# A hybrid attention and retention block on one Trainium2 core: small transposes and products of ones replaced by DMA, first MLP blocks reordered

## The chip, the cores and the metric

The kernel runs on one core of one Trainium2 chip. The metric is the device time of one execution in microseconds (us). TensorE (PE) multiplies, VectorE (DVE) and ScalarE (ACT) work on rows, GpSimd (POOL) and SyncE (SP) here only issue DMAs.

## The reference, cut to what matters

One layer, 256 tokens, model width 2048, float32. An indexer with 16 heads of 64 picks 64 keys for every query of an attention with 16 heads; beside it runs a retention with 8 heads; both are gated, merged, projected, and an MLP of width 8192 follows.

```python
h = rms_norm(x, ln1_g[l])
proj = h @ w_in[l]                       # queries, keys, values, indexer, retention, gates ga, gb
...
logits = jnp.einsum('bqhd,bsd->bqhs', iqb, ik)                     # indexer
score = jnp.einsum('bqh,bqhs->bqs', iwb, jax.nn.relu(logits))
_, idx = lax.top_k(score, topk)
...
merged = jax.nn.sigmoid(ga) * (o_attn @ w_up_attn[l]) + jax.nn.sigmoid(gb) * (o_ret @ w_up_ret[l])
x = x + merged @ w_out[l]
h2 = rms_norm(x, ln2_g[l])
x = x + jnp.square(jax.nn.relu(h2 @ w_ff1[l])) @ w_ff2[l]
```

## The kernel before, in words

All weights stream through once, in a fixed order (`stream`, `use`). A weight item is a tile of 2 x 128 rows and 512 columns. ScalarE rounds it to a shorter float format (`whi`, L363) and VectorE subtracts to get the rest (`wlo`, L364). Each float32 product is three TensorE products (L409 to L411): high by high, high by low, low by high. `ahead` issues loads on SP's queue eight items before their use and splits two or three items before; `lows` lists the subtractions made so far, `late["split"]` the newest rounding.

Tokens lie in two tiles (t = 0, 1) of 128. `run_block` goes through the 16 steps (k) of a block of 512 columns; at each step `step()` lets all small pieces of work in the list `work` advance by one `yield`. So the number of yields in a generator sets how many steps lie between its parts. The scheduler of the language then places instructions on each engine in its own order; `tc.issue_after(i)` keeps an instruction behind i on its engine.

The blocks in order: keys of the attention together with the indexer's first block, the indexer's other two (`I`), values (`AV`), queries (`AQ`), retention queries and keys (`RQ`, `RK`), the gates `GA` and `GB` (in seven products of quarter blocks instead of eight, `PRODUCTS`, with `SUMS` of weight tiles made on VectorE and `TIED` naming those that are kept behind a subtraction; between them stand items of other blocks), `RG`, `RV`, `UR`, the output projection `O`, then the MLP: `F1` for the first group of 1024 hidden columns as two plain blocks (1, then 0), and for seven more groups as seven products each, between items of `F2`.

A tile is turned (transposed) in two ways. On TensorE by a product with the identity, as in `indexer` (L579, L584) and `last_rows` (L1139), with an eviction from PSUM. Or by DMA (`turned`): ScalarE splits float32 into two planes of 16 bits (L451), SP issues a transposing DMA (L453), and ScalarE joins the planes some steps later (L457).

Three places spread one number per token over all partitions or columns. `forms_h` builds sums of the two token tiles for the gates; it needs the ratio of the tiles' norm factors, `rho`, as a row on every partition: a diagonal matrix times ones (L764). `spread_rs` does the same for the factors of the second norm (L1181), used by `scaled_rows`, which scales the transposed rows of blocks 0 to 2 of `O`. The last block's rows go through `last_rows`, which scales them on ScalarE before the transposes. `next_norm` then splits them into `xf`, which the `F1` blocks read, and `forms` builds four more combinations and holds the tile `rawc` for it, into which `F2` weights are loaded afterwards.

The attention's `attend_tile` waits for `keys`, made at the end of `indexer`. The gates' values are made by sigmoids on ScalarE (L500); `gated` (L904) multiplies them with the attention's projection. A sigmoid of a dummy tile (L835) stands after the second `RQ` block.

Of the kernel before, what the change touches and what calls it, by code (L numbers as in the profile page):

```python
# [10 lines left out]
F32 = mybir.dt.float32  # L11
# [66 lines left out]
def stream():  # L78
# [25 lines left out]
    for g in range(NG):  # L104
# [15 lines left out]
        15: ("C", "A", 0), 18: ("C", "A", 1), 22: ("D", "C", 0), 25: ("D", "C", 1)}  # L120
TIED = {(("GA", 0), ("A", "B", 1)): 4, (("GA", 0), ("B", "C", 0)): 8, (("GA", 1), ("B", "C", 0)): 2, (("GA", 1), ("B", "C", 1)): 4, (1, ("B", "C", 0)): 4, (1, ("C", "A", 0)): 4}
F2_HALVES = (1, 0)
# [17 lines left out]
PAIR = (("UR", 0), ("UR", 1))  # L140
PARTS = ((0, 1), (2,), (3,))

BESIDE = {"GA": "UA", "GB": "RG"}
# [18 lines left out]
def block_kernel(ctx, tc, cst, rot, xt, gains, w, x, ret_gn_g, ret_gn_b, out):  # L162
# [29 lines left out]

    W_NORM, W_SOFT, W_GN, W_CROSS, W_ROWS, W_LAST, W_QUERY, W_PROBS = 3, 5, 7, 8, 7, 6, 5, 5
    n_stg, n_mid, n_sm = 8, {"ep": 12, "e4": 20}, 24
# [64 lines left out]
    for key, name, _, nk, _, n in stream():  # L259
        B[key] = (nk, n)  # L260
        for h in range(nk // KC):
            at[key, h] = (w[off:off + KC * P * n].rearrange("(p c n) -> p c n", p=P, c=KC), n)
            if name != "w_ff2" and key[0] not in QUARTERS and key[0] not in BESIDE.values() and key not in PAIR:
# [183 lines left out]
    def turned(src, halves, wait, tied=False, dst=None, mirror=None):  # L447

        mirror = src if mirror is None else mirror
        with tc.issue_after(late["split"]) if tied else nullcontext():  # L450
            nc.scalar.activation(planes(halves), interleaved(src), AF.Copy)  # L451
        yield
        nc.sync.dma_start_transpose(mirror.bitcast(U16).rearrange("p (c r) -> p c r", r=P), halves.bitcast(U16))  # L453
        for _ in range(wait):
            yield
        with tc.issue_after(late["split"]):
            nc.scalar.activation(interleaved(halves if dst is None else dst), planes(mirror), AF.Copy)  # L457

# [100 lines left out]

    iqs = ep.tile([P, T, IW], F32, tag="big", name="iqs")  # L560
    for i in range(3):
        ps = run_block(("I", i), of(hT)) if i else psI
        for t in range(T):
            evict(iqs[:, t, i * IN:(i + 1) * IN], ps[t], t)
    mb = []

    def indexer():
        ik2 = mid([P, T, 2, ID])
# [3 lines left out]
        iqT = ep.tile([P, IH // 2, S], F32, tag="a1", name="iqT")  # L572
        ikT = mid([P, S])
        yield
        for c in range(0, IH // 2, 2):
            ps = psum_t()
            for a in range(2):
                for t in range(T):
                    nc.tensor.transpose(ps[:, (2 * a + t) * P:(2 * a + t + 1) * P], iqs[:, t, (c + a) * P:(c + a + 1) * P], ident)  # L579
            nc.scalar.activation(iqT[:, c:c + 2, :], ps.rearrange("p (a s) -> p a s", a=2), AF.Copy)  # L580
            yield
# [3 lines left out]
        nc.vector.tensor_copy(ikT, ps[:, :S])  # L585
        yield
        yield
# [16 lines left out]
        sc = [mid([P, (t + 1) * P]) for t in range(T)]  # L604
        for t, h0 in ((0, 0), (1, 0), (1, IH // 2)):
            heads = logits(t, h0)
            yield
            for h, src in enumerate(heads, h0):
                if h == 0:
                    nc.vector.tensor_scalar(sc[t], src, iw[:, t, h:h + 1], None, op0=ALU.mult)  # L610
                else:
                    nc.vector.scalar_tensor_tensor(sc[t], src, iw[:, t, h:h + 1], sc[t], op0=ALU.mult, op1=ALU.add)
                if h % 4 == 3:
                    yield
# [3 lines left out]
        for i in range(TOPK // 8):  # L618
            m8 = [small(8) for _ in range(T)]
            for t in range(T):  # L620
                nc.vector.max(m8[t], sc[t])
            for t in range(T):
                nc.vector.match_replace(sc[t], m8[t], sc[t], GONE)
            yield
            if i % 2:
                yield
        for t in range(T):
# [132 lines left out]
    def forms_h():  # L760

        diag, ps = stage((P, P)), psum_t()
        nc.vector.tensor_scalar(diag, ident, rho, None, op0=ALU.mult)
        nc.tensor.matmul(ps[:, :P], warm, diag, start=True, stop=True)  # L764
        nc.scalar.activation(ratio, ps[:, :P], AF.Copy)
        yield
# [13 lines left out]
        for half in range(2):  # L780
            whole(X2[:, half], 1, half)
            yield
            for q in range(0, HK, 4):
# [28 lines left out]
    for which, key in ((0, "RQ"), (1, "RK")):  # L812
        for i in range(2):
            last = (which, i) == (1, 0)
            ps = run_block((key, i), of(hT), before=(lambda k: scaled(k // 4 - 1) if k in (4, 8, 12) else None) if last else None)
            if which == i == 0:
# [9 lines left out]
                late["rtab"] = e2.tile([P, 2, T, 2, RD], F32, name="rtab")  # L826
                late["rawc"] = px.tile([P, 2, KC, BN], F32, tag="big2", name="rawc")
                nc.gpsimd.dma_start(late["rtab"].rearrange("p a b c d -> p (a b c d)"), rot)
            for t in range(T):
                work.append(rotated(evicted(ps[t], t), t, which, i))  # L830
            if which == i == 0:
                work.append(forms_h())
            if (which, i) == (0, 1):
                with tc.issue_after(late["split"]):
                    nc.scalar.activation(small(8), warm[:, :8], AF.Sigmoid)  # L835
            if last:
# [62 lines left out]
    def gated(u, done, ready):  # L899

        for t, i in list(ready):
            if done[i] == DK // HC:
                z = ready.pop((t, i))
                nc.vector.tensor_tensor(z, acc[2 * u + i][t], z, op=ALU.mult)  # L904
                nc.gpsimd.dma_start(mgd[:, t, (2 * u + i) * BN:(2 * u + i + 1) * BN], z)
# [200 lines left out]

    crossed = [0] * 3

    def cross(i, t):

        for _ in range(2 + t):
            yield
# [12 lines left out]

    def last_rows(i):

        xs = []
        for t in range(T):
            a = stage()  # L1130
            nc.scalar.activation(a, x2[:, t, i * BN:(i + 1) * BN], AF.Copy, scale=rs[:, t:t + 1])
            xs.append(a)
        yield
        half, c0 = divmod(4 * i, HK)
        for k in range(0, 4, 2):
            ps = psum_t()
            for c in range(2):
                for t in range(T):
                    nc.tensor.transpose(ps[:, (2 * c + t) * P:(2 * c + t + 1) * P], xs[t][:, (k + c) * P:(k + c + 1) * P], ident)  # L1139
            for c in range(2):  # L1140
                nc.scalar.activation(xr[half][:, :, c0 + k + c, :], ps[:, c * S:(c + 1) * S].rearrange("p (t s) -> p t s", t=T),
                                     AF.Copy, scale=g2[:, 4 * i + k + c:4 * i + k + c + 1])
            yield

    def next_norm(i):

        yield from scaled_rows(i) if i < 3 else last_rows(i)
        yield
# [24 lines left out]
    def spread_rs():  # L1173

        diag = stage((P, S))
        for t in range(T):
# [4 lines left out]
        nc.tensor.matmul(ps[:, :S], warm, diag, start=True, stop=True)  # L1181
        nc.scalar.activation(across, ps[:, :S], AF.Copy)
        late["across"] = across.rearrange("p (t s) -> p t s", t=T)
# [24 lines left out]
    def norm_end():  # L1208
# [7 lines left out]
        nc.vector.tensor_tensor(q2, rec, rec, op=ALU.mult)  # L1216

    work.append(norm_end())

# [26 lines left out]
    ys = {}  # L1246
    for i in (1, 0):
        ps = run_block(("F1", i), lambda k, t: form(blocks[k // HK][t], k % HK))
        for t in range(T):
            ys[t, i] = squared(stage(), ps[t])  # L1250
            if i:
# [105 lines left out]
```

## Time and profile before

| what | value |
|---|---|
| time, median of 3 runs | 1575.37 us (1575.32 to 1575.76) |
| the profiled execution | 1575.43 us |
| its span, first to last instruction | 1573.7 us |
| granted TensorE clock | 1.000 |
| instructions | 19357 |
| HBM read, written | 323.24 MB, 27.26 MB |

In the profile's rows, an engine's busy time comes with its share of the span; a group of instructions has its line in the kernel, what it writes and reads, its count, its busy time and the mean of one in ns, and the idle time of the engine before it with what ended it. Timeline rows begin with the start in us from the span's start and the length. The row of a stretch (A:B) gives its length, then the busy time of PE, weight loading, DVE, ACT and POOL with their counts, the clock, the DMA engines' share and GB/s. Rows of DMA issues end with the median time in us from issue to landing.

### The profile page before, as it was taken

What the parts mean: (1) busy time and instruction counts of PE and PEld (TensorE: products, weight loads), DVE (VectorE), ACT (ScalarE), POOL (GpSimd) and SP (SyncE); (2) the same over time, 40 slices, a digit from 0 to 9 for tenths busy, and PEclk for the clock granted to TensorE, in tenths of its full rate; (3) what the DMA queues carried; (4) which work ended last, traced back from release to release, by engine and by line L of the source; (5) the groups of instructions that cost most, each with busy time, mean ns of one, the idle gap of its engine ahead of it and who ended that gap; (6) DMA issues with size and microseconds to landing.
All of it is one profiled execution on the core that took longest, in us unless ns stands there. A gap on an engine that the chain in (4) does not pass through costs nothing.

```text
span 1573.7 us, 19357 instructions
## 1 busy us (share of the span) xinstructions
PE 1567.0 (100%) x7140; PEld 1304.7 (83%) x7140; DVE 1317.2 (84%) x1489; ACT 1134.4 (72%) x1350; POOL 90.7 (6%) x135
## 2 busy tenths in 40 slices
PE   9999999999999999999999999999999999999999
PEld 8988888888888888888888888888888888888887
DVE  5678889899999898688665689898989898989885
ACT  7657887766666666477676778787878686878783
POOL 0000000000000001302000000101000000000000
PEclk9999999999999999999999999999999999999999
DMA  9746667966565755968769785978778787979684
GB/s 333 238 149 195 197 187 247 281 208 246 205 243 210 271 183 190 334 213 292 226 231 289 225 282 172 266 225 281 227 261 234 239 255 241 267 241 266 216 211 163
DMA packets 147616, 371.45 MB, mean 236 GB/s; under 512 B 86976, under 2 KB 93760, under 8 KB 111936
## 3 DMA queue, kind: packets, MB, share of 16 engines
q1 hardware_dynamic: 130240, 328.63, 62.4%
q0 software_dynamic: 14256, 35.14, 9.6%
q10 hardware_dynamic: 3024, 6.44, 1.1%
q8 instruction: 56, 0.92, 0.2%
q14 instruction: 40, 0.33, 0.1%
HBM read 323.24 MB, written 27.26 MB: 223 GB/s over the span
## 4 chain that ended last, share of the span: by engine, by line
PE 98%; DVE 1%; DMA 0%; issue 0%; ACT 0%; ACTq 0%
PE pm L409 12%; PE pm L410 12%; PE pm L411 12%; PE pf L410 11%; PE pf L411 11%; PE pf L409 11%; PE pq L410 9%; PE pq L411 9%; PE pq L409 9%; PE pa L410 0%; PE pa L409 0%; PE pa L411 0%; PE pa L965 0%; DMA xts<-in_xt_dram 0%; DVE wlo L364 0%
## 5 line engine op out<-in xcount | busy, mean ns | idle before, releaser
L364 DVE TENSOR_TENSOR wlo<-raw,whi 128x1024 fp32r<-128x1024 f32 (+2 forms) x544 | 644.1, 1202 | 161.9 <-ACT whi L363 150.5
L363 ACT ACTIVATE whi<-raw 128x1024 fp32r<-128x1024 f32 (+2 forms) x544 | 560.7, 1039 | 282.1 <-PE pm L411 113.9
L409 PE MATMUL pm<-whi,act 128*128 128x512 f32 (+1 forms) x800 | 308.1, 386 | 1.4 <-ACT act L474 1.4
L410 PE MATMUL pm<-wlo,act 128*128 128x512 f32 (+1 forms) x800 | 306.6, 383 | 0.2 <-DVE wlo L364 0.2
L411 PE MATMUL pm<-whi,act 128*128 128x512 f32 (+1 forms) x800 | 306.2, 383 | 0.0
L410 PE MATMUL pf<-wlo,act 128*128 128x512 f32 (+1 forms) x768 | 299.6, 390 | 0.0
L411 PE MATMUL pf<-whi,act 128*128 128x512 f32 (+1 forms) x768 | 298.3, 388 | 0.0
L409 PE MATMUL pf<-whi,act 128*128 128x512 f32 (+1 forms) x768 | 297.8, 388 | 0.0
L364 DVE TENSOR_TENSOR wlo<-rawc,whi 128x1024 fp32r<-128x1024 f32 x176 | 215.1, 1222 | 37.9 <-ACT whi L363 36.4
L363 ACT ACTIVATE whi<-rawc 128x1024 fp32r<-128x1024 f32 x176 | 185.9, 1056 | 62.9 <-PE pf L411 26.1
L353 DVE TENSOR_TENSOR raw<-raw,raw 128x2048 f32<-128x2048 f32 x88 | 201.4, 2288 | 0.6
L409 PEld LDWEIGHTS pm<-whi,act 128*128 128x128 f32 x800 | 150.3, 188 | 28.6 <-ACT act L474 1.6
L411 PEld LDWEIGHTS pm<-whi,act 128*128 128x128 f32 x800 | 150.2, 188 | 27.8 <-DVE act L475 0.2
L410 PEld LDWEIGHTS pm<-wlo,act 128*128 128x128 f32 x800 | 150.4, 188 | 27.4 <-DVE wlo L364 1.2
L410 PEld LDWEIGHTS pf<-wlo,act 128*128 128x128 f32 x768 | 144.2, 188 | 32.9 <-DVE wlo L364 3.6
L409 PEld LDWEIGHTS pf<-whi,act 128*128 128x128 f32 x768 | 144.2, 188 | 29.8
L411 PEld LDWEIGHTS pf<-whi,act 128*128 128x128 f32 x768 | 144.3, 188 | 29.0
L410 PE MATMUL pq<-wlo,xf 128*128 128x512 f32 x392 | 152.7, 389 | 0.0
L411 PE MATMUL pq<-whi,xf 128*128 128x512 f32 x392 | 152.7, 389 | 0.0
L409 PE MATMUL pq<-whi,xf 128*128 128x512 f32 x392 | 152.6, 389 | 0.0
L1305 POOL DMA_DIRECT2D sums<-halves x56 | 48.2, 965 | 741.7 <-ACT halves L1304 740.1
L410 PEld LDWEIGHTS pq<-wlo,xf 128*128 128x128 f32 x392 | 73.6, 188 | 15.5 <-DVE wlo L364 0.2
(223 smaller groups left out, 1603.6 us busy)
## 6 DMA issues: line engine op xcount, KB each, us to landing
raw<-in_w_dram SPq DMA_DIRECT2D x188, 1024.0 KB, 6.0
rawc<-in_w_dram SPq DMA_DIRECT2D x88, 1024.0 KB, 5.3
sums<-halves POOLq DMA_DIRECT2D x56, 256.0 KB, 7.1
raw<-in_w_dram SPq DMA_DIRECT2D x8, 736.0 KB, 5.5
raw<-in_w_dram SPq DMA_DIRECT2D x7, 512.0 KB, 7.0
raw<-in_w_dram SPq DMA_DIRECT2D x8, 368.0 KB, 7.2
stg<-in_x_dram SPq DMA_DIRECT2D x8, 256.0 KB, 7.7
mgd<-stg POOLq DMA_DIRECT2D x8, 256.0 KB, 5.5
```

The source lines that it names most:

```text
L353: nc.vector.tensor_tensor(one, one, two, op=ALU.add)
L363: late["split"] = nc.scalar.activation(a, src, AF.Copy).ins
L364: lows.append(nc.vector.tensor_tensor(b, src, a.bitcast(F32), op=ALU.subtract).ins)
L409: nc.tensor.matmul(d, h, hi, start=first, stop=False, skip_group_check=skip)
L410: nc.tensor.matmul(d, h, lo, start=False, stop=False, skip_group_check=skip)
L411: nc.tensor.matmul(d, l, hi, start=False, stop=last, skip_group_check=skip)
L1305: nc.gpsimd.dma_start(sums[:, t, i * BN:(i + 1) * BN], z, accum_op=ALU.add)
```

## The change

1. The indexer's queries are turned by DMA: new generators `index_tile`, one for each token tile and half, started as soon as the `I` blocks that hold the half are out. `indexer` then takes the logits of tile 1's first half first, waits for what has been turned (`turned_iq`), keeps its VectorE work behind the newest weight subtraction, and takes two steps for each round of selection.
2. `rho` is written to DRAM and read back into all partitions by DMA; `forms_h` multiplies after both additions.
3. The dummy sigmoid is gone, and the products of `gated` are tied behind the newest subtraction.
4. `spread_rs` goes through DRAM by two DMAs and waits four steps.
5. The last block of `O` is turned like the others (`cross`), `last_rows` is gone, and the first two `F1` blocks run in four parts: block 1 up to row 11, block 0 up to row 3, the rest of block 1, the rest of block 0.
6. One more sum of weights of the second MLP group is tied.

```diff
-TIED = {..., (1, ("B", "C", 0)): 4, (1, ("C", "A", 0)): 4}
+TIED = {...,
+        (1, ("A", "B", 1)): 4, (1, ("B", "C", 0)): 4, (1, ("C", "A", 0)): 4}
+F1_PARTS = ((1, (0, 1, 2)), (0, (0,)), (1, (3,)), (0, (1, 2, 3)))
...
+        if key == ("F1", 0):
+            use += [(("F1", i), h, s) for i, part in F1_PARTS for h in part for s in range(KC // HC)]
...
+    rhod = dp.tile([1, P], F32, name="rhod")
+    nc.gpsimd.dma_start(rhod.rearrange("o p -> p o"), rho)
...
+    def index_tile(t, half):
+        for _ in range(t if half else 4 + 2 * t):
+            yield
+        if "iqT" not in late:
+            late["ik2"] = mid([P, T, 2, ID])
+            late["iqT"] = ep.tile([P, IH // 2, S], F32, tag="a1", name="iqT")
+        c = IH // 4
+        dst = late["iqT"][:, half * c:(half + 1) * c, t * P:(t + 1) * P]
+        yield from turned(iqs[:, t, half * BN:(half + 1) * BN], stage(), W_INDEX + t if half else W_CROSS, dst=dst)
+        turned_iq.add((t, half))
...
+        if i:
+            work.extend(index_tile(t, i - 1) for t in range(T))
...
-        for c in range(0, IH // 2, 2):
-            ps = psum_t()
-            for a in range(2):
-                for t in range(T):
-                    nc.tensor.transpose(ps[:, (2 * a + t) * P:(2 * a + t + 1) * P], iqs[:, t, (c + a) * P:(c + a + 1) * P], ident)
-            nc.scalar.activation(iqT[:, c:c + 2, :], ps.rearrange("p (a s) -> p a s", a=2), AF.Copy)
+        for _ in range(3):
             yield
...
-        for t, h0 in ((0, 0), (1, 0), (1, IH // 2)):
+        for t, h0, needs in ((1, 0, {(1, 0)}), (0, 0, {(0, 0), (0, 1)}), (1, IH // 2, {(1, 1)})):
+            while not needs <= turned_iq:
+                yield
+            for _ in range(0 if t else 2):
+                yield
...
             yield
-            if i % 2:
-                yield
+            yield
...
-        diag, ps = stage((P, P)), psum_t()
-        nc.vector.tensor_scalar(diag, ident, rho, None, op0=ALU.mult)
-        nc.tensor.matmul(ps[:, :P], warm, diag, start=True, stop=True)
-        nc.scalar.activation(ratio, ps[:, :P], AF.Copy)
...
+                nc.gpsimd.dma_start(ratio, rhod.to_broadcast([P, P]))
                 nc.gpsimd.dma_start(late["rtab"].rearrange("p a b c d -> p (a b c d)"), rot)
...
-            if (which, i) == (0, 1):
-                with tc.issue_after(late["split"]):
-                    nc.scalar.activation(small(8), warm[:, :8], AF.Sigmoid)
...
-                nc.vector.tensor_tensor(z, acc[2 * u + i][t], z, op=ALU.mult)
+                with tc.issue_after(lows[-1]):
+                    nc.vector.tensor_tensor(z, acc[2 * u + i][t], z, op=ALU.mult)
...
-        for _ in range(2 + t):
+        for _ in range((2 if i < 3 else 1) + t):
             yield
...
-        yield from scaled_rows(i) if i < 3 else last_rows(i)
+        yield from scaled_rows(i)
...
-        diag = stage((P, S))
-        for t in range(T):
-            nc.vector.tensor_scalar(diag[:, t * P:(t + 1) * P], ident, rs[:, t:t + 1], None, op0=ALU.mult)
-        for _ in range(3):
-            yield
-        ps, across = psum_t(), stage((P, S))
-        nc.tensor.matmul(ps[:, :S], warm, diag, start=True, stop=True)
-        nc.scalar.activation(across, ps[:, :S], AF.Copy)
+        spread, across = dp.tile([1, S], F32, name="spread"), stage((P, S))
+        nc.gpsimd.dma_start(spread.rearrange("o (t p) -> p (o t)", p=P), rs)
+        nc.gpsimd.dma_start(across, spread.to_broadcast([P, S]))
+        for _ in range(4):
+            yield
...
+    for t in range(T):
+        work.append(cross(3, t))
     work.append(norm_end())
...
-    for i in (1, 0):
-        ps = run_block(("F1", i), lambda k, t: form(blocks[k // HK][t], k % HK))
+    up = {}
+    for i, part in F1_PARTS:
+        up[i] = run_block(("F1", i), lambda k, t: form(blocks[k // HK][t], k % HK), ps=up.get(i),
+                          k0=part[0] * KC, k1=(part[-1] + 1) * KC)
+        if part[-1] < DK // KC - 1:
+            continue
```

More of the change, by code (lines that the diff above doesn't have):

```diff
@@ L120 @@
         15: ("C", "A", 0), 18: ("C", "A", 1), 22: ("D", "C", 0), 25: ("D", "C", 1)}
-TIED = {(("GA", 0), ("A", "B", 1)): 4, (("GA", 0), ("B", "C", 0)): 8, (("GA", 1), ("B", "C", 0)): 2, (("GA", 1), ("B", "C", 1)): 4, (1, ("B", "C", 0)): 4, (1, ("C", "A", 0)): 4}
+TIED = {(("GA", 0), ("A", "B", 1)): 4, (("GA", 0), ("B", "C", 0)): 8, (("GA", 1), ("B", "C", 0)): 2, (("GA", 1), ("B", "C", 1)): 4,
+        (1, ("A", "B", 1)): 4, (1, ("B", "C", 0)): 4, (1, ("C", "A", 0)): 4}
 F2_HALVES = (1, 0)
@@ L190, in block_kernel @@
     banks(**ONE)
-    W_NORM, W_SOFT, W_GN, W_CROSS, W_ROWS, W_LAST, W_QUERY, W_PROBS = 3, 5, 7, 8, 7, 6, 5, 5
+    W_NORM, W_SOFT, W_GN, W_CROSS, W_ROWS, W_LAST, W_QUERY, W_PROBS, W_INDEX = 3, 5, 7, 8, 7, 6, 5, 5, 5
     n_stg, n_mid, n_sm = 8, {"ep": 12, "e4": 20}, 24
@@ L262, in block_kernel @@
             at[key, h] = (w[off:off + KC * P * n].rearrange("(p c n) -> p c n", p=P, c=KC), n)
-            if name != "w_ff2" and key[0] not in QUARTERS and key[0] not in BESIDE.values() and key not in PAIR:
+            if name != "w_ff2" and key[0] not in QUARTERS and key[0] not in BESIDE.values() and key not in PAIR and key[0] != "F1":
                 use += [(z, h, s) for s in range(KC // HC) for z in {("AK", 0): (), ("I", 0): (("AK", 0), key)}.get(key, (key,))]
@@ L456, in turned @@
         with tc.issue_after(late["split"]):
-            nc.scalar.activation(interleaved(halves if dst is None else dst), planes(mirror), AF.Copy)
+            if dst is None or len(dst.shape) == 2:
+                nc.scalar.activation(interleaved(halves if dst is None else dst), planes(mirror), AF.Copy)
+            else:
+                nc.scalar.activation(dst.bitcast(U16).rearrange("p c (i h) -> p h c i", h=2), planes(mirror).rearrange("p h (c i) -> p h c i", i=P), AF.Copy)
     def turn_in(act, k0, t, src, tile_for, wait, land=W_CROSS, tied=False, mirror=None):
@@ L560, in block_kernel @@
     iqs = ep.tile([P, T, IW], F32, tag="big", name="iqs")
+    turned_iq = set()
+    def index_tile(t, half):
[8 more added lines that the diff above has]
+        turned_iq.add((t, half))
     for i in range(3):
@@ L564, in block_kernel @@
             evict(iqs[:, t, i * IN:(i + 1) * IN], ps[t], t)
+        if i:
+            work.extend(index_tile(t, i - 1) for t in range(T))
     mb = []
     def indexer():
-        ik2 = mid([P, T, 2, ID])
+        ik2, iqT = late["ik2"], late["iqT"]
         iw = cp.tile([P, T, IH], F32, name="iw")
@@ L608, in indexer @@
             for h, src in enumerate(heads, h0):
[L609 to L612, printed above, removed]
+                with tc.issue_after(lows[-1]):
+                    if h == 0:
+                        nc.vector.tensor_scalar(sc[t], src, iw[:, t, h:h + 1], None, op0=ALU.mult)
+                    else:
+                        nc.vector.scalar_tensor_tensor(sc[t], src, iw[:, t, h:h + 1], sc[t], op0=ALU.mult, op1=ALU.add)
                 if h % 4 == 3:
@@ L619, in indexer @@
             m8 = [small(8) for _ in range(T)]
-            for t in range(T):
-                nc.vector.max(m8[t], sc[t])
+            with tc.issue_after(lows[-1]):
+                for t in range(T):
+                    nc.vector.max(m8[t], sc[t])
             for t in range(T):
@@ L624, in indexer @@
             yield
-            if i % 2:
-                yield
+            yield
         for t in range(T):
@@ L782, in forms_h @@
             yield
+        for half in range(2):
             for q in range(0, HK, 4):
@@ L903, in gated @@
                 z = ready.pop((t, i))
-                nc.vector.tensor_tensor(z, acc[2 * u + i][t], z, op=ALU.mult)
+                with tc.issue_after(lows[-1]):
+                    nc.vector.tensor_tensor(z, acc[2 * u + i][t], z, op=ALU.mult)
                 nc.gpsimd.dma_start(mgd[:, t, (2 * u + i) * BN:(2 * u + i + 1) * BN], z)
@@ L1105, in both @@
         nc.vector.tensor_tensor(lo, src, hi.bitcast(F32), op=ALU.subtract)
-    crossed = [0] * 3
+    crossed = [0] * 4
     def cross(i, t):
-        for _ in range(2 + t):
+        for _ in range((2 if i < 3 else 1) + t):
             yield
@@ L1124, in scaled_rows @@
             nc.vector.scalar_tensor_tensor(z, z, g2[:, 4 * i + k:4 * i + k + 1], late["across"], op0=ALU.mult, op1=ALU.mult)
[L1126 to L1143, printed above, removed]
     def next_norm(i):
-        yield from scaled_rows(i) if i < 3 else last_rows(i)
+        yield from scaled_rows(i)
         yield
@@ L1173, in spread_rs @@
     def spread_rs():
-        diag = stage((P, S))
-        for t in range(T):
-            nc.vector.tensor_scalar(diag[:, t * P:(t + 1) * P], ident, rs[:, t:t + 1], None, op0=ALU.mult)
-        for _ in range(3):
+        spread, across = dp.tile([1, S], F32, name="spread"), stage((P, S))
+        nc.gpsimd.dma_start(spread.rearrange("o (t p) -> p (o t)", p=P), rs)
+        nc.gpsimd.dma_start(across, spread.to_broadcast([P, S]))
+        for _ in range(4):
             yield
-        ps, across = psum_t(), stage((P, S))
-        nc.tensor.matmul(ps[:, :S], warm, diag, start=True, stop=True)
-        nc.scalar.activation(across, ps[:, :S], AF.Copy)
         late["across"] = across.rearrange("p (t s) -> p t s", t=T)
@@ L1216, in norm_end @@
         nc.vector.tensor_tensor(q2, rec, rec, op=ALU.mult)
+    for t in range(T):
+        work.append(cross(3, t))
     work.append(norm_end())
@@ L1246, in block_kernel @@
     ys = {}
-    for i in (1, 0):
-        ps = run_block(("F1", i), lambda k, t: form(blocks[k // HK][t], k % HK))
+    up = {}
[4 more added lines that the diff above has]
+            continue
         for t in range(T):
-            ys[t, i] = squared(stage(), ps[t])
+            ys[t, i] = squared(stage(), up[i][t])
             if i:
```

1 line of the change is left out of this document (removed).

## The prediction

> **What bounds the kernel now.** I read the engines' shares first, then the chain that ended last, then stretches of the timeline around each place that the change touches.
>
> ```profile
> PE 1567.0 (100%) x7140; PEld 1304.7 (83%) x7140; DVE 1317.2 (84%) x1489; ACT 1134.4 (72%) x1350; POOL 90.7 (6%) x135
> PE 98%; DVE 1%; DMA 0%; issue 0%; ACT 0%; ACTq 0%
> ```
>
> TensorE is busy for the whole span and carries 98% of the chain. A busy TensorE may still be waiting inside a modelled end, so I also looked at the spacing of starts. Away from the places below, a 512-column product starts every 0.227 us with nothing between. So an instruction taken off TensorE is worth its slot, as long as the operand that replaces it arrives in time. And every late operand costs its lateness in full. These slots go away, as the chain prices them:
>
> ```profile
> 78.50 0.44 PE pt L579 x4
> ...
> 83.98 0.44 PE pt L579 x4
> ...
> 239.08 0.22 PE pt L764 x2
> ...
> 893.33 0.43 PE pt L1181 x2
> ...
> 913.76 0.22 PE pt L1139 x2
> ...
> 914.21 0.66 PE pt L1139 x6
> ```
>
> **The change part by part.**
>
> *Products taken off TensorE.* Four groups of four transposes of the indexer's queries (first and last shown) at 0.44 make 1.76. The product of ones for the ratio is 0.22, the one for the row scales 0.43, the last rows' transposes 0.22 + 0.66 = 0.88. Together 3.29 us. A second, smaller saving hangs on them, seen in the spacing before and after the product of ones:
>
> ```profile
> 891.58 0.39 PE L409 MATMUL pm<-whi,act 128*128 128x512 f32 x1
> ...
> 892.94 0.39 PE L409 MATMUL pm<-whi,act 128*128 128x512 f32 x1
> ...
> 894.05 0.40 PE L409 MATMUL pm<-whi,act 128*128 128x512 f32 x1
> ...
> 895.22 0.39 PE L411 MATMUL pm<-whi,act 128*128 128x512 f32 x1
> ```
>
> Before it six starts take 1.36 us (0.227 each, and six make one step of a block's loop: 1.36 us); after it five take 1.17 (0.234). Some ten products run 0.006 slower behind such a break, 0.06 us. I count five breaks that go: 0.3, between 0 and 0.4. Sum of this part: -3.6, between -3.3 and -3.7.
>
> *Indexer's queries by DMA.* For each of four tiles come a plane split on ScalarE, a DMA transpose on SP's queue and a joining copy on ScalarE; four evictions go.
>
> ```profile
> L451 ACT ACTIVATE halves<-stg x46: 1028/1042/1060, 52.8 to 1525.2; 128x1024 uint16<-128x1024 uint16 x46
> L457 ACT ACTIVATE halves<-stg x46: 1339/1358/1380, 62.3 to 1533.4; 128x1024 uint16<-128x1024 uint16 x46
> L580 ACT ACTIVATE iqT<-pt x4: 582/590/599, 79.0 to 85.0; 128x512 f32<-128x512 f32 x4
> DMA to landing us min/median/max: 3.1/5.2/11.9
> 76.50:92.50 16.00, 16.00 (x104) 13.26 (x103) 8.25 (x13) 9.54 (x15) 0.00 (x0) 1.00 0.53 180
> L637 ACT ACTIVATE keys<-kT x1: 1047/1047/1047, 127.7 to 127.7; 128x1024 fp32r<-128x1024 f32 x1
> L679 PE MATMUL pa<-kT,stg x32: 270/275/276, 141.5 to 221.2; 128*128 128x128 f32 x32
> ```
>
> ScalarE gains 4 x (1.04 + 1.36) - 4 x 0.59 = 7.2 us, spread over two blocks; in the second it is busy 9.54 of 16 us, and half of the new work falls in the first. The transposes (the fourth row is their landing) have 5 or more steps of 1.36 = 6.8 us in the value block: the median 5.2 fits; the longest, 11.9, would hold ScalarE 5 us and with it the next weight split. SP's weight loads stand behind each transpose, but are asked for eight items ahead, some 20 us. Selection starts from a reordered list (logits of the second half first) and takes 16 steps for 12. I count the keys 3 to 4 steps later, about 5 us; they are made at 127.7 and first used at 141.5, a cover of 13. Taken: 0; ends 0 and +5.
>
> *Ratio by DMA.* Its write goes out right after the first norm, and the read back stands on POOL's queue ahead of the rotary table.
>
> ```profile
> L828 POOL DMA_DIRECT2D rtab<-in_rot_dram x1: 702/702/702, 227.3 to 227.3; - x1
> L741 DVE TENSOR_TENSOR stg<-stg,rtab x8: 687/690/693, 248.2 to 306.7; 128x512 f32<-128x512 f32 x8
> ```
>
> The table was issued at 227.3 and used at 248.2, so a read ahead of it delays nobody, and the multiplications by the ratio, which follow the same block's end and now stand one addition later, have nearly the same cover of 20 us. VectorE loses a small scaling and ScalarE a copy, both off the path. Taken 0; ends -0.3 (two such pieces) and +0.7 (the table's own issue, were the ratio late by as much).
>
> *Sigmoid's early call removed; gate products tied.* The early call only brought in ScalarE's function table. Its load now falls before the first sigmoid of the gates.
>
> ```profile
> 258.35 1.99 ACT L363 ACTIVATE whi<-raw 128x1024 fp32r<-128x1024 f32 x2
> 260.36 1.28 ACT L835 ACT_TABLE_LOAD   x1
> 261.65 0.21 ACT L835 ACTIVATE small<-warm 128x8 f32<-128x8 f32 x1
> ...
> 369.07 1.34 ACT L500 ACTIVATE stg<-stg,r 128x512 f32<-128x512 f32 x2 [0.15 <-DVE stg L871]
> 370.63 1.06 ACT L363 ACTIVATE whi<-raw 128x1024 fp32r<-128x1024 f32 x1 [0.23 <-PE pf L411]
> ...
> 373.34 1.06 ACT L363 ACTIVATE whi<-raw 128x1024 fp32r<-128x1024 f32 x1 [0.30 <-PE pq L411]
> ...
> 371.75 1.29 DVE L904 TENSOR_TENSOR stg<-pf,stg 128x512 f32<-128x512 f32 x2
> 372.94 2.35 DVE L364 TENSOR_TENSOR wlo<-raw,whi 128x1024 fp32r<-128x1024 f32 x2
> ...
> 374.45 0.50 PE L409 MATMUL pq<-whi,act 128*128 128x512 f32 x1 [0.52 <-ACT whi L363]
> ```
>
> This is TensorE's largest single wait: the split of 373.34 ends at 374.40 and the product starts at 374.45, about 0.68 us after it could. Behind it stand two gate products (L904) that delayed two weight subtractions on VectorE. If the ties put the subtractions first, 0.7 to 0.8 us go. But the tie names the newest subtraction when the product is written down; counting the items, that one had begun before 366, so the tie may not bind here. If the order stays, the load pushes the sigmoids from 369.07 by 1.28; the three splits after them (one is left out of the rows) then run back to back from 371.9 at about 1.0 each, and the last ends at 374.9, not 374.40: +0.5. Ends -0.8 and +0.5, about equally far; taken 0. In the row of the load nothing else is lost: the split before it ends at 260.34, the load begins at 260.36 and the next call at 261.65. The Trainium skill prices a switch of tables higher (ScalarE: Activation LUTs, What ACT_TABLE_LOAD costs): 1.283 us of load and about 1.38 us of drain. The trace agrees with the first figure and shows no second; with both, this term would be an estimated +1.9 and the whole sum -1.8. I go by the row.
>
> *Row scales spread by DMA.* Here two small DMAs on POOL's queue, the second waiting for the first, replace two VectorE scalings, a product and a copy.
>
> ```profile
> 892.04 0.17 DVE L1200 COPY rs<-small 128x2 f32<-128x2 f32 x1
> 894.22 3.26 DVE L1124 SCALAR_TENSOR_TENSOR xr<-xr,gT,stg 128x256 f32<-128x256 f32 x8
> ...
> 899.37 1.29 DVE L1105 TENSOR_TENSOR xf<-xr,xf 128x512 fp32r<-128x512 f32 x2 [0.69 <-ACT xf L1104]
> ...
> 908.37 0.39 PE L409 MATMUL pm<-whi,xf 128*128 128x512 f32 x1
> ...
> sgd<-stg POOLq DMA_DIRECT2D x8, 256.0 KB, 2.6
> ...
> rqT<-rqkd POOLq DMA_DIRECT2D x4, 256.0 KB, 11.0
> ```
>
> The scales are there at 892.2. No row shows a DMA this small; the nearest on this queue land in 2.6 us (quiet) and 11.0 (many queued). Two give 897.4 to 914.2. POOL's queue is empty here, so I stay near the low row, 3 to 4 each: 899. The first eight multiplications then start 5 us later than 894.22, and the rows that ended at 900.7 end at 905.5 for a first use at 908.37. Their users wait if the scales land after about 902, and then us for us. Taken 0; ends 0 and +12.
>
> *First MLP blocks in four parts.* Rows 12 to 15 come four steps (5.4 us) later in the order, so their DMA transposes (two more on SP) fit: cross starts by step 2, joins by step 10, is scaled (4 x 0.48 on VectorE) and split by step 12; used at step 16. ScalarE gives back two scalings and four evictions for two splits and two joins. What is late next is the first block's hidden rows:
>
> ```profile
> 924.31 0.33 SPq L329 DMA_DIRECT2D rawc<-in_w_dram  x1
> ...
> 948.58 0.69 DVE L434 TENSOR_TENSOR act<-stg,act 128x512 fp32r<-128x512 f32 x1 [0.62 <-ACT act L433]
> ...
> 955.55 0.39 PE L409 MATMUL pf<-whi,act 128*128 128x512 f32 x1
> 961.28 0.50 PE L410 MATMUL pf<-wlo,act 128*128 128x512 f32 x1
> ```
>
> They were ready at 949.3 and first read at 955.55: 6.2 us of cover, of which four steps take 5.4, leaving 0.8. On VectorE two weight subtractions (2.35 in the row of 372.94) may get ahead of them: taken 0, ends 0 and 2.35 - 0.8 = +1.6. The Strassen-like forms start some 7 steps (9.5 us) later; the load that now leaves at 924.31 waits for them on SP till about 934, the loads behind it too; its data is split after 950, so 5 to 6 us of landing fit. The new tie for the sums of the second group aims at a lateness like that of 961.28 (0.29 instead of 0.227 after its neighbour, plus a slower stretch): -0.1; ends -0.2 and 0.
>
> **Sum.** -3.6 + 0 + 0 + 0 + 0 + 0 - 0.1 = -3.7. The profiled execution took 1575.43 us (span 1573.7 and 1.7 around it), 0.06 above the median of 1575.37. 1575.43 - 3.7 = 1571.7.
>
> **The rivals.**
> *A, new waits eat the gain.* One or two of the covers of 0.8 to 3 us are too thin: the hidden rows at 955 (up to +1.6), the table load in the old order (+0.5), the scales (some us past 902), a slow transpose (up to +5). For: VectorE is busy 84% of the span, so what is late stays late for a while. Against: the splits stand two to three items ahead. Typical: two of the first three, +1.6, 1573.3.
> *B, slower.* The scales' two DMAs land late. Price: every us past 902. Net zero is at 905.7; slower by 0.2% (3.15 us, about what a measurement of this kernel tells from no change) from 908.9 on, which needs 8.3 us for each DMA. At the slow row, 11.0 each, it is +12: 1583.7. For: the write is 256 pieces of four bytes. Against: an idle queue.
> *C, the slots are not TensorE's.* If the transposes filled waits for weights, taking them away gains nothing: 1575.4. Against: no wait is listed there, and the starts around them are 0.23 apart.
> *D, more than forecast.* The ties clear the wait at 374: 1571.7 - 0.8 = 1570.9.
> *E, the table load costs ScalarE twice its row.* A pause as long as the load itself, 1.28, follows it before the sigmoids: the term of the gates is 0.5 + 1.28 = +1.8, the time 1573.5. Against: the next call 0.01 after the load at 261.65; 0.03. It is the drain of the Trainium skill (ScalarE: Activation LUTs, What ACT_TABLE_LOAD costs).
>
> **How the numbers follow.** Forecast with D: 0.63 (D 0.15 of it). A: 0.24, E: 0.03, C: 0.04, all within 0.2% of before. B: 0.06, here counted as slower whole. Faster 0.63, same 0.31, slower 0.06. Predicted 1571.7, the likeliest. The range goes down to D, 1570.8, and up through A with its larger ends to 1574.2; B lies outside.
>
> **What would show it.** TensorE with 28 transposes or products fewer; the starts at 78 to 85 evenly 0.227 apart; a table load just before a sigmoid near 366; the first xf product no later than 905; no wait at the first F2 product near 952. Wrong if the chain shows POOL's DMA or VectorE's xr for over 1 us around 900, or ScalarE held by a transpose near 85.

## The result: 13 us slower, and the profile after

The changed kernel takes 1588.64 us (median of five; 1586.85 to 1589.25) against 1575.37 before: ratio 1.0082, 95% interval 1.0071 to 1.0093. That is +13.3 us where -3.7 was forecast; rival B, the late row scales, came to pass. In the changed kernel the rounding is L367, the subtraction L368, the products L413 to L415, the scaling L1142, the split into `xf` L1122 and L1123, and the two new DMAs L1175 and L1176 (in some of the kernels below the last ones stand a line or more further down).

The page of the changed kernel, engines and chain:

```profile
PE 1567.0 (99%) x7112; PEld 1302.7 (82%) x7112; DVE 1316.4 (83%) x1490; ACT 1141.0 (72%) x1349; POOL 93.2 (6%) x139
PE 80%; issue 11%; DVE 3%; DMA 3%; ACT 2%; POOL 0%; SPq 0%; ACTq 0%; POOLq 0%; DVEq 0%
```

The 28 instructions are gone from TensorE, as announced. But the chain is no longer TensorE's alone: DMA and VectorE have 3% each, and 11% is "issue", which is mostly POOL with nothing to do before its DMA (153.6 us) and not a cost. The list of waits names the place (in all, times, longest, us):

```profile
PE pm L414 <- DVE wlo L368: 13.0, 2, 12.8
POOL stg L1176 <- DMA spread<-rs: 10.0, 1, 10.0
DVE xr L1142 <- DMA stg<-spread: 14.7, 1, 14.7
ACT xf L1122 <- DVE xr L1142: 15.8, 3, 15.0
```

POOL waits 10.0 for the first DMA, VectorE 14.7 for the second, and TensorE 12.8 in its turn. What TensorE waits for is neither the scales nor `xf`, but a weight subtraction. The chain in the window from 885 to 935 gives the order (start, us, what):

```profile
890.11 10.19 DMA spread<-rs
900.32 0.47 issue
900.80 8.31 DMA stg<-spread
909.14 3.25 DVE xr L1142 x8
912.40 1.66 DVE xf L1123 x3
...
914.81 1.15 DVE wlo L368
916.00 0.79 PE pm L414
```

VectorE's timeline there shows why a weight comes last. Only two subtractions stand between the scales' copy and the scalings; the next ones are queued behind the instruction that waits:

```profile
889.64 0.17 DVE L1196 COPY rs<-small 128x2 f32<-128x2 f32 x1
890.54 1.23 DVE L368 TENSOR_TENSOR wlo<-raw,whi 128x1024 fp32r<-128x1024 f32 x1 [0.72 <-ACT whi L367]
893.25 1.23 DVE L368 TENSOR_TENSOR wlo<-raw,whi 128x1024 fp32r<-128x1024 f32 x1 [1.48 <-ACT whi L367]
909.14 3.25 DVE L1142 SCALAR_TENSOR_TENSOR xr<-xr,gT,stg 128x256 f32<-128x256 f32 x8 [14.67 <-DMA stg<-spread]
912.32 2.49 DVE L1123 TENSOR_TENSOR xf<-xr,xf 128x512 fp32r<-128x512 f32 x4
914.72 2.36 DVE L368 TENSOR_TENSOR wlo<-raw,whi 128x1024 fp32r<-128x1024 f32 x2
```

And TensorE's, with the granted clock (the number ahead of the DMA share) in stretches of the same window:

```profile
902.78 0.39 PE L413 MATMUL pm<-whi,act 128*128 128x512 f32 x1
916.00 0.79 PE L414 MATMUL pm<-wlo,act 128*128 128x512 f32 x1 [12.83 <-DVE wlo L368]
...
917.01 0.63 PE L413 MATMUL pm<-whi,act 128*128 128x512 f32 x1
917.44 0.63 PE L414 MATMUL pm<-wlo,act 128*128 128x512 f32 x1
...
919.84 0.40 PE L414 MATMUL pm<-wlo,act 128*128 128x512 f32 x1
920.08 0.39 PE L415 MATMUL pm<-whi,act 128*128 128x512 f32 x1
920.31 0.40 PE L413 MATMUL pm<-whi,xf 128*128 128x512 f32 x1
```

```profile
900.00:902.00 2.00, 2.00 (x10) 1.65 (x10) 0.00 (x0) 0.00 (x0) 0.56 (x1) 1.00 0.43 29
906.00:912.00 6.00, 0.00 (x0) 0.00 (x0) 2.86 (x8) 1.15 (x3) 0.00 (x0) 0.50 0.09 9
916.00:918.00 2.00, 2.00 (x5) 1.61 (x6) 2.00 (x4) 2.00 (x3) 0.00 (x0) 0.50 0.39 90
920.00:922.00 2.00, 2.00 (x11) 1.60 (x10) 2.00 (x3) 1.06 (x1) 0.00 (x0) 1.00 0.60 139
```

No product starts between 902.78 and 916.00, and the next eight come 0.427 apart instead of 0.227, at a granted clock of 0.50. Over the 50 us from 900 the starts lie 14.8 us further apart than at an even 0.227; in the kernel before it was 0.2. So this one place costs 14.6 us, of which 13.0 is the wait and 1.6 the half clock. Behind it the profile has three smaller waits that the kernel before has not: starts 0.73, 1.19 and 0.92 us apart at 981.55, 1029.79 and 1550.02, some 2.2 us together.

### The profile page after: what moved, and what is told of

It reads as the page before. It is cut to its first block, busy times and chain, and to the rows that moved or that the text cites. A ratio compares the mean times of both kernels' runs of the same rounds, so it can differ in the third digit from the quotient of the medians.

```text
span 1587.5 us, 19313 instructions
## 1 busy us (share of the span) xinstructions
PE 1567.0 (99%) x7112; PEld 1302.7 (82%) x7112; DVE 1316.4 (83%) x1490; ACT 1141.0 (72%) x1349; POOL 93.2 (6%) x139
## 4 chain that ended last, share of the span: by engine, by line
PE 80%; issue 11%; DVE 3%; DMA 3%; ACT 2%; POOL 0%; SPq 0%; ACTq 0%; POOLq 0%; DVEq 0%
PE pf L414 10%; PE pf L413 10%; PE pf L415 10%; PE pq L414 8%; PE pm L414 8%; PE pq L413 8%; PE pq L415 8%; PE pm L415 8%; PE pm L413 8%; DVE wlo L368 2%; ACT whi L367 1%; DMA rawc<-in_w_dram 1%; DMA spread<-rs 1%; DMA stg<-halves 1%; DVE raw L357 1%
## 5 line engine op out<-in xcount | busy, mean ns | idle before, releaser
L368 DVE TENSOR_TENSOR wlo<-raw,whi 128x1024 fp32r<-128x1024 f32 (+2 forms) x544 | 643.8, 1200 | 161.9 <-ACT whi L367 150.5
L367 ACT ACTIVATE whi<-raw 128x1024 fp32r<-128x1024 f32 (+2 forms) x544 | 560.2, 1039 | 275.6 <-PE pm L415 108.7
L413 PE MATMUL pm<-whi,act 128*128 128x512 f32 (+1 forms) x800 | 308.2, 386 | 1.0 <-ACT act L481 0.7
L415 PE MATMUL pm<-whi,act 128*128 128x512 f32 (+1 forms) x800 | 306.8, 384 | 0.0
L413 PE MATMUL pf<-whi,act 128*128 128x512 f32 (+1 forms) x768 | 298.2, 389 | 0.6 <-ACT act L437 0.5
L415 PE MATMUL pf<-whi,act 128*128 128x512 f32 (+1 forms) x768 | 298.3, 388 | 0.0
L368 DVE TENSOR_TENSOR wlo<-rawc,whi 128x1024 fp32r<-128x1024 f32 x176 | 214.9, 1221 | 39.2 <-ACT whi L367 37.8
L367 ACT ACTIVATE whi<-rawc 128x1024 fp32r<-128x1024 f32 x176 | 185.8, 1056 | 63.8 <-PE pf L415 25.8
L413 PEld LDWEIGHTS pm<-whi,act 128*128 128x128 f32 x800 | 150.7, 188 | 28.8 <-ACT act L481 0.9
L415 PEld LDWEIGHTS pm<-whi,act 128*128 128x128 f32 x800 | 150.7, 188 | 28.0 <-DVE act L482 0.2
L413 PEld LDWEIGHTS pf<-whi,act 128*128 128x128 f32 x768 | 144.2, 188 | 31.1 <-ACT act L437 1.0
L415 PEld LDWEIGHTS pf<-whi,act 128*128 128x128 f32 x768 | 144.3, 188 | 29.6 <-DVE act L438 0.4
L413 PE MATMUL pq<-whi,xf 128*128 128x512 f32 x392 | 152.6, 389 | 0.0
L415 PE MATMUL pq<-whi,xf 128*128 128x512 f32 x392 | 152.6, 389 | 0.0
L413 PEld LDWEIGHTS pq<-whi,xf 128*128 128x128 f32 x392 | 73.6, 188 | 15.3
```

The lines of the kernel that those rows point to most:

```text
L367: late["split"] = nc.scalar.activation(a, src, AF.Copy).ins
L368: lows.append(nc.vector.tensor_tensor(b, src, a.bitcast(F32), op=ALU.subtract).ins)
L413: nc.tensor.matmul(d, h, hi, start=first, stop=False, skip_group_check=skip)
L415: nc.tensor.matmul(d, l, hi, start=False, stop=last, skip_group_check=skip)
```

## Experiments

Each gives the median and, where it was timed in rounds, the ratio to the kernel before on the same chip (1575.42 to 1575.47 us) with its 95% interval. "The ones" is the product of ones that spread the row scales before.

**One part undone: the ones back in the changed kernel.**

```
-        spread, across = dp.tile([1, S], F32, name="spread"), stage((P, S))
-        nc.gpsimd.dma_start(spread.rearrange("o (t p) -> p (o t)", p=P), rs)
-        nc.gpsimd.dma_start(across, spread.to_broadcast([P, S]))
+        diag = stage((P, S)) ... nc.tensor.matmul(ps[:, :S], warm, diag, ...) ...
```

> The changed kernel with the row scales spread by a product of ones again; all else as changed. Theory W (the scales' two DMAs, 19.0 us from the scales to the landing, hold VectorE 14.7 us, TensorE runs out of weight subtractions for 13.0 us and then runs at half clock for 3.8 us, 1.7 us lost): the 14.7 us go, 0.5 comes back for the product, so 1588.6 - 14.2 = 1574.4 or less, with no wait of over 1 us between 880 and 925. Theory O (another part is at the root and the wait only shows there, as the indexer's transposes or the four-part order shift the schedule): 1584 or more, with a wait of several us elsewhere.

1572.90 us, 0.9984 (0.9975 to 0.9993). Without the two DMAs the rest of the change gains 2.6 us, and of the three later waits only one is left, 0.5 us by the starts at 968. So the loss goes with the two DMAs; whether the stall itself brings the later waits is not shown.

**The same part alone, in the kernel before:** the two DMAs in place of the ones.

> The kernel before with nothing but the row scales spread by two DMAs on POOL's queue. Theory W: 1575.4 + 14.7 - 0.5 = about 1589.5, with VectorE waiting 13 to 16 us for the spread tile and the clock at 0.50 in the stretch behind it. Theory O: under 1578, because the other parts that make the scales late are not there.

1587.60 us, 1.0075 (1.0062 to 1.0087): +12.1, with a wait of 11.3 us on VectorE, somewhat less of both than theory W had. The part needs no help from the other parts to do its harm. Its landings were 10.8 and 4.4 us, by the list of DMA issues of that run:

```profile
stg<-spread POOLq DMA_DIRECT2D x1, 128.0 KB, 4.4
spread<-rs POOLq DMA_DIRECT2D x1, 1.0 KB, 10.8
```

**Another queue:** in the changed kernel both `nc.gpsimd.dma_start` of the spread become `nc.sync.dma_start`.

> The changed kernel with the scales' two DMAs issued on SP's queue, not POOL's. Theory Q (POOL's way of issuing makes them slow: 10.2 and 8.3 us there): both land in 2 to 4 us each, VectorE waits under 2 us, time 1572 to 1576. Theory P (256 pieces of four bytes into DRAM, and a read of 128 copies behind a write, are slow on any queue): landings of 7 us or more each, 1584 to 1592; SP's loads stand behind the second wait, which may add some us.

1581.73 us, 1.0039 (1.0026 to 1.0052). The time lies outside both ranges; the landings are those of theory P. The write is as slow on SP's queue, so POOL's issue is not what takes the time:

```profile
stg<-spread SPq DMA_DIRECT2D x1, 128.0 KB, 7.1
spread<-rs SPq DMA_DIRECT2D x1, 1.0 KB, 10.5
```

It lost 6.9 us less than the changed kernel, and the trace shows two differences: the read landed 1.2 us faster, and a third subtraction (at 895.72) stood ahead of the waiting scaling. How much each is worth this run cannot tell. That made the order a suspect of its own.

**The transfers without their users:** the kernel before keeps the ones and issues both DMAs beside them, the read cut to 8 columns.

> The kernel before, products of ones kept; the write of the scales to DRAM and a read of 8 of them are added on POOL's queue into a tile that nobody uses. Theory W (the cost is VectorE's wait): 1575.4 within 0.5. Theory T (the small pieces clog the DMA engines, weight loads are late, as the 20 to 29 GB/s between 894 and 902 in the changed kernel may say): 1578 or more, with a wait for weights after 892. Either way the landings show if 8 to 10 us per DMA is what such pieces take here.

1575.54 us, 1.0002 (0.9993 to 1.0011), with a write that landed after 12.4 us. Nine of the eleven runs took 1575.0 to 1576.3, two 1578.1 and 1578.6; the profile is of the slowest, and its largest new wait, 1.8 us, stands at 1202; what made these two longer is not shown. So where nobody waits for them, the transfers cost the usual run no time; the 14.6 us are what waits for them. But they are not free for the DMA engines, and theory T was right in that. The weight loads issued between 885 and 905 landed like this in the kernel before and in this run:

```profile
DMA to landing us min/median/max: 4.8/4.9/5.1
DMA to landing us min/median/max: 5.3/8.2/13.4
```

The load of 13.4 us left at 894.05, while the write was on its way (892.3 to 904.6). A load is asked for eight items ahead, and TensorE did not wait for a weight between 890 and 1199.

**What a small write costs by itself:** pairs of a write and a read on POOL's queue, in the kernel before.

```
+    for np_, wd, turn in ((P, 2, True), (P, 1, False), (P, 2, False), (P, 8, False), (16, 1, False), (1, 8, False)):   # twice
+            nc.gpsimd.dma_start(<DRAM row, np_ pieces of wd floats>, b[:np_, :wd])
+            nc.gpsimd.dma_start(c, d[:, :8].to_broadcast([P, 8])); b = c
```

> The kernel before, with twelve pairs of unused DMAs on POOL's queue while it is otherwise idle (from about 740 us): a write to DRAM and a read back of 8 columns into 128 partitions, each waiting for the one ahead. The writes differ in their pieces: 256 of 4 bytes (as the row scales), 128 of 4, 128 of 8, 128 of 32, 16 of 4, one of 32; the six kinds twice over. Theory P (a write pays for each small piece): about 10 us for 256 pieces, 8 for the three kinds with 128 whatever their bytes, 3 for 16 and for one. Theory L (a write pays its way through the weight loads, however many pieces it has): all six alike, 6 to 11 us. Reads back 4 to 6 us in both. The time stays at 1575.5 within 0.2% in both, since nobody waits for these transfers.

The list of DMA issues of that run (KB each, median us to landing). The 1.0 KB rows are 256 pieces of 4 bytes and 128 of 8, 0.5 KB is 128 of 4, 4.0 KB is 128 of 32, 0.1 KB is 16 of 4, and 0.0 KB one of 32:

```profile
pr<-small POOLq DMA_DIRECT2D x3, 1.0 KB, 7.0
pr<-small POOLq DMA_DIRECT2D x2, 0.5 KB, 9.7
pr<-small POOLq DMA_DIRECT2D x2, 4.0 KB, 10.2
pr<-small POOLq DMA_DIRECT2D x2, 0.1 KB, 4.0
pr<-small POOLq DMA_DIRECT2D x2, 0.0 KB, 4.9
pr<-csb POOLq DMA_DIRECT2D x1, 1.0 KB, 7.7
```

One by one, in the order of the list in the code, the writes took 7.7, 9.2, 6.2, 5.6, 2.8 and 3.9 us the first time, and 9.4, 10.2, 7.0, 14.9, 5.2 and 5.8 the second (the very first left at 35.9 us, ahead of the stretch that was meant). In each round every write of 128 or 256 pieces took longer than both of few pieces, and among those of 128 the bytes show no trend. That speaks for the theory of pieces. With only two of a kind the spread is wide, and 256 is not seen to be dearer than 128.

The time was expected unchanged and was not: one run of 1592.44. TensorE stopped once for 12.0 us. The chain there passes through a transposing DMA on SP's queue that took 22.3 us (TensorE's waits; the chain; the landings of the two transposes of that place, in the kernel before and in this run):

```profile
PE pm L409 <- ACT act L433: 12.0, 1, 12.0
826.02 22.33 DMA stg<-stg
DMA to landing us min/median/max: 8.2/8.4/8.7
DMA to landing us min/median/max: 21.4/21.9/22.3
```

This transpose was issued 2.1 us later than in the kernel before, and TensorE was 2.1 us behind already. So the gates' loads, which stand on POOL's queue behind the probe and left up to 77 us later than before, are not what held it. While the transpose was on its way, a read of the probe and its slowest write (14.9 us) were too. The 2.1 us arose near 750, behind another transpose of 13.6 us (7.0 before), and 2.6 us followed at half clock. With one run it is not shown that the small pieces alone slowed these transposes, but it is the same slowness of other DMAs as in the run before.

**Fewer pieces in place:** the changed kernel, the scales first turned into two rows.

```
+        for _ in range(3): yield
+        nc.tensor.transpose(ps[:T, :P], rs, ident)
+        nc.scalar.activation(two[:T, :], ps[:T, :P], AF.Copy)
-        nc.gpsimd.dma_start(spread.rearrange("o (t p) -> p (o t)", p=P), rs)
+        nc.gpsimd.dma_start(spread, two[:T, :])
...
```

> The changed kernel, but the row scales are first turned into two rows on TensorE (one small transpose three steps behind the norm, a copy on ScalarE), written to DRAM as two pieces of 512 bytes instead of 256 of 4, and read back as before. Theory P: the write lands in 2.5 to 4 us and the read in 4 to 8, the scales are there at about 901 to 905 though they leave 4 us later than in the changed kernel; most of the stall goes: 1573 to 1578. Theory L: 10 and 8 again from 894: 913, and 1588 to 1592.

1573.03 us, 0.9986 (0.9977 to 0.9995). The same 1 KB in two pieces, 1.3 us later, and the stall is gone; VectorE waited 1.0 us for it. The other DMAs of the place are quick again as well: weight loads issued between 885 and 905 land in 4.8 to 5.0 us and transposes in 3.6 to 3.8, where the slowest of the changed kernel took 13.5 and 14.6. That the read, unchanged but for its order behind the write, fell from 8.3 to 3.2 fits this; a run that changes the read alone was not made.

```profile
stg<-spread POOLq DMA_DIRECT2D x1, 128.0 KB, 3.2
spread<-stg POOLq DMA_DIRECT2D x1, 1.0 KB, 3.4
```

**The order on VectorE, first try:** `range(4)` behind the DMAs becomes `range(13)`.

> The changed kernel with the scalings of the rows 13 steps behind the two DMAs, not 4, so that some four more weight subtractions stand ahead of them on VectorE. Theory W (two losses: the scales are late, and VectorE's order holds the weights behind them): TensorE no longer stops at 903 for a weight subtraction; it stops at 906 for the first xf rows, which come 4 us after the scales' landing at 909, some 7 us, and the half clock after it costs 1.6 more: 1572.9 + 8.6 = 1581.5 (1579 to 1583.5). Theory Q (only the order is at fault): 1573 to 1576. Theory D (only the landing counts, the order is nothing): 1587 to 1589.

1584.62 us, 1.0057 (1.0044 to 1.0070): between the theories, and outside the range. The wait for a weight stayed (`wlo`, 8.6 us at 903), because the scheduler of the language placed the scalings behind the same two subtractions all the same; only the later scalings were spread out, with a subtraction after every three or four. So this run moved less than I meant it to.

**The order, second try:** ten steps, and `with tc.issue_after(lows[-1]):` around the scaling.

> The changed kernel with the scalings of the rows ten steps behind the DMAs and also tied behind the newest weight subtraction, so that VectorE's order has four subtractions, not two, between the row scales and the first scaling (the wait of 13 steps had not changed that order: the scheduler pulled the scalings ahead again). The landings stay 10 and 8 us. Theory W (the stall has two parts): TensorE no longer stops for a weight subtraction before 905; it stops at about 906 for the first xf rows, which come 3 to 4 us after the scales' landing at about 909: 7 us, and 1.6 for the half clock after it, 1581.5 (1580 to 1583.5). Theory Q (only the order was at fault): 1573 to 1575. Theory D (only the landing counts): 1587 to 1589.

1583.22 us, 1.0051 (1.0038 to 1.0063), in the range of the theory of two losses. Four subtractions now stand ahead, and TensorE waits for `xf`, not for a weight; a landing 2 us later than in the changed kernel still cost less:

```profile
PE pm L413 <- ACT xf L1122: 7.9, 1, 7.9
DVE xr L1143 <- DMA stg<-spread: 11.3, 1, 11.3
```

**The same DMAs, one block earlier:** the scales are taken from two blocks of `O` instead of three (the last norm divides them out), the scalings keep their place by the tie, and the spread scales get a buffer of their own.

```
-        if i == 2:
+        if i == 1:
             ...
-            nc.vector.tensor_reduce(ss, ss2...[:, :, :3], ...); rsqrt(ss, T, 1.0 / (3 * BN))
+            nc.vector.tensor_reduce(ss, ss2...[:, :, :2], ...); rsqrt(ss, T, 1.0 / (2 * BN))
             work.append(spread_rs())
+        if i == 2:
             for k in range(3): work.append(next_norm(k))
```

> The changed kernel with the row scales taken from the first two blocks of O instead of the first three (the last norm divides them out again), so that the same two DMAs leave one block, 21.8 us, earlier; the scalings stay in their place by a tie. Theory P with W (the change lost only because 18 us of landings had 12 us of cover): the landings are still 8 to 12 and 4 to 9 us long, VectorE and TensorE wait for none of them, and all slots are gained: the 1572.9 of the kernel with the ones put back, less 0.43 for that product, 1572.4 (1571.6 to 1573.2). Rival X (the two DMAs or the moved scalings cost something else in O or F1): over 1575.

1572.71 us, 0.9983 (0.9975 to 0.9992). The DMAs are as slow as ever, and nobody waits for them: among VectorE's and TensorE's waits there is none for `spread`.

```profile
across<-spread POOLq DMA_DIRECT2D x1, 128.0 KB, 6.6
spread<-rs POOLq DMA_DIRECT2D x1, 1.0 KB, 9.8
```

**The other parts alone, in the kernel before.** The indexer's queries by DMA:

> The kernel before with one part alone: the indexer's queries turned by DMA. By the sum of the prediction: 1.76 us of transposes and up to 0.2 of slow pace: 1575.46 - 1.9 = 1573.6. Rival G (the last transposes land late and the logits, or a weight split behind the waiting ScalarE, hold TensorE for 1 to 2 us, as the profile with the ones put back shows at 81 to 84): 1574.3 to 1575.5.

1573.92 us, 0.9990 (0.9982 to 0.9999): -1.5. The first MLP blocks in four parts, with the last rows by DMA (the kernel of this run leaves out the new tie of the sums, which its expectation names; the kernel of the next run has it):

> The kernel before with one part of the change alone: the first MLP blocks in four parts, the last rows by DMA transposes and scaled like the others, and the new tie of the sums. The scales still come by the product of ones. By the sum of the prediction: 0.88 us of transposes and 0.1 of slow pace go, 1575.46 - 1.0 = 1574.5. Rival G (what is late next takes it back: hidden rows near 968 to 982, 0.5 to 1 us): 1575.0 to 1575.6.

1574.75 us, 0.9995 (0.9986 to 1.0004): -0.7. The ratio by DMA, the sigmoid's early call away, the gate products tied, and the tie of the sums:

> The kernel before with the rest of the change but the row scales: the ratio by DMA, the early sigmoid away, the gate products tied. By the sum of the prediction: one slot of 0.22 and nothing else, 1575.2. Rival D (the ties and the missing table load clear the waits at 261 and 373, as the changed kernel's spacing has it: 0.5 and 0.45): 1574.3. Rival E (the load of the table before the gates' sigmoids holds the splits): 1576 to 1577.

1574.75 us, 0.9996 (0.9987 to 1.0005): -0.7. The intervals of the last two hold no change as well. The three add up to -2.9, where the changed kernel with the ones back has -2.6. With the +12.1 of the row scales alone the sum is +9.2, and the changed kernel has +13.3: its stall is longer (starts 13.2 us apart at the stop, not 9.9), and it has the later waits of 2.2 us.

## Why the prediction was wrong, by its own steps

**The step that failed is the term of the row scales.** It took "3 to 4 each", close to the nearest quiet row of 2.6 us, and measured 10.2 and 8.3. The rows it leaned on were of another kind: 256 KB transfers. The prediction named the difference, "256 pieces of four bytes", and set it aside for an idle queue. The empty queue did not help: 10.5 on SP's, 9.8 a block earlier, 6 to 15 for 128 or 256 pieces in the probe, and 3.4 once the pieces were two. Its upper end of two landings of 11.0 was the nearer one. That the write also slows the loads and transposes beside it was in none of the steps.

**The price was mis-sized too.** "Their users wait if the scales land after about 902, and then us for us" gives 7 us for a landing at 909.1. It cost 14.6. The tied kernel shows what is right: TensorE needs `xf` at 905.5, and `xf` came 2.4 us after the landing, 911.1 to 913.5; so 903.1 is the latest landing, and 6.0 of the loss are us for us. The rest:

- 2.5 us: TensorE stopped at 903.0, not 905.5, since a weight subtraction ran out first, queued behind VectorE's wait.
- 4.5 us: it went on at 916.0 instead of 909.1 + 2.4 = 911.5, since all eight scalings and the splits came ahead of that subtraction.
- 1.6 us: half the clock for eight products after the pause.

Together 14.6. The prediction weighed VectorE's order for the gates and the hidden rows, but did not ask which subtractions stand behind the scalings.

**The other terms held.** The three kernels without the stall take 1572.7 to 1573.0, inside the range and 1.0 to 1.3 above the 1571.7 forecast.

- *Products off TensorE*, -3.6: part alone by part alone, the indexer's transposes gave -1.5 for 1.76, the last rows' -0.7 for 0.88 (an interval that holds no change). In the profiled run of the indexer's part the last product of all starts 1.75 us earlier than before, 0.2 of which came in the first 50 us. Rival C is out.
- *Indexer's queries*, 0: no wait at 81 to 84 in the changed kernel. With the ones back one transpose took 8.9 us, and TensorE waited 0.9 and 0.5 for the indexer's own key, which was behind it; so the end of +5 was too high, but not empty.
- *Sigmoid and ties*, 0: rather -0.5, the -0.7 of the part alone less its slot of 0.22. The table load now stands before the gates' sigmoids, and the wait of 374 shrank all the same, as rival D had it, but by 0.2 us and not 0.8. The larger gain is at 261, behind the early call, where 0.6 us went, which no step had counted. The tie of the sums, -0.1, gained nothing to be seen: the late subtraction of 961 was on time, and one as late stood at 977. ScalarE in the changed kernel:

```profile
366.74 1.28 ACT L509 ACT_TABLE_LOAD   x1
368.04 1.34 ACT L509 ACTIVATE stg<-stg,r 128x512 f32<-128x512 f32 x2
369.28 1.04 ACT L367 ACTIVATE whi<-raw 128x1024 fp32r<-128x1024 f32 x1
```

  The sigmoid begins 0.02 us after the load ends, so rival E, a pause behind it, is out. The Trainium skill (ScalarE: Activation LUTs, What ACT_TABLE_LOAD costs) has a drain of about 1.38 us beside the load; no run here shows it.
- *Ratio by DMA*, 0: nobody waited. Its write of 128 pieces landed in 8.5 us, nearly as slow as that of the scales, with some 180 us of cover.
- *Four parts*, 0: a wait of 0.3 us at 982 in the changed kernel, of 0.4 at 967 in the one with early scales and of 0.5 at 961 in the part alone, within its end of +1.6.

What stays open is a smaller thing: by 51 us TensorE is 0.3 to 1.0 us behind the kernel before in the profiles of the changed kernel and of its variants with the DMAs, level with it where the ones are back, and between 0.2 ahead and 0.1 behind in the kernels with one of the other parts. Why is not shown.

## What to carry to other kernels

Before a product of ones or a transpose is traded for a trip through DRAM, count the pieces of the write: one value per partition is 128 or more of them, and here such writes took 6 to 12 us, once 15, on POOL's queue and on SP's alike. It did no harm where the value was known a block ahead, and was dear where the value was made just in time; moving the producer earlier, or first making few long pieces, kept the gain. Look at the other DMAs beside such a write as well: here loads and transposes issued next to it took some two to four times as long. And ask of a new wait what stands behind it on that engine: here the work that waited in line stopped TensorE before the waited-for data did.

## What the hardware showed that I had not expected

A write of 1 KB from one value per partition took 9.8 to 12.4 us on the way to DRAM in seven runs (the scales), and 3.4 us as two rows. The Trainium skill (DMA: Bandwidth & Descriptors, Anatomy of one DMA) gives about 2.0 us and the bytes over 436e3 for a DMA of this queue, an estimated 2.0 us here. The two rows took 1.4 us more than that, the 256 pieces five times as long, so the measurement decides. While the write was on its way, loads and transposes beside it were slow too: in the changed kernel a weight load that left at 891.8 landed after 13.5 us and a transpose that left at 894.2 after 14.6, where the kernel before has 5.1 and 3.8 at most. Beside the two rows nothing of the kind is seen. The runs show that this goes with the pieces, not what in the DMA engines makes it so.

After a pause of 13 us the clock was granted at 0.50 from 906 on, and for 3.6 us after the restart (916.0 to 919.6); in the five other runs with such a pause it was 4.2 to 6.0 us. The Trainium skill (TensorE: Matmul & The Clock Gate, Part 1) says that an idle window of about 3.4 us halves the clock and a busy one restores it; the trace agrees in that the half clock never ended sooner, 3.6 us at the least. The shortest stop that halved it here was 4.8 us between two starts (SP's queue); one of 2.2 us (the unused transfers) did not. So a long wait of TensorE has a surcharge, here 1.6 us.
